# A hybrid decoder layer on one core: spills of a block's split input one transfer at a time, and weight sums paused during three attention projections

## The chip, the cores and the metric

The kernel runs on one core of one Trainium2 chip. Its time is device microseconds (us) of that core; a comparison goes by the median of several runs. PE is TensorE (matmuls), DVE is VectorE, ACT is ScalarE, POOL is GpSimd, SP is SyncE, which here does nothing but issue DMA transfers. POOL issues transfers as well: those that add to what lies at the destination.

## The reference, cut to what matters

One layer of a decoder on 2048 prompt rows and 64 sample rows of width 1024, in float32:

```
h    = rms_norm(x)
proj = h @ w_in                      # q, k, v | z, x/B/C, dt | b, c, u
o_a  = rms_norm(dilated attention(q, k, v))       # three branches, merged
y_b  = rms_norm(ssd_scan(silu(conv(x/B/C)), dt) * silu(z))
y_c  = rms_norm(b * conv(c * u))
x    = x + rms_norm(concat(o_a, y_b, y_c) @ w_out)
f    = relu(rms_norm(x) @ w_mlp_up)**2 @ w_mlp_down
x    = x + rms_norm(f)
# outputs: x of prompt and sample; k and v rows, ssd state, conv states of both
```

## The kernel before, in words

**Products.** Every float32 product of the projections is made of three matmuls on split operands: a value is written as hi + lo (hi rounded to a short format, lo the rest), and hi·lo + hi·hi + lo·hi are added up in one PSUM bank (`mm3`, L282). Weights are split when loaded: ACT writes `whi`, POOL or DVE writes `wlo` (`split_w`). The input rows are split too, once per block: 16 tiles of 128x576 per block (`hi0` to `hi7`, `lo0` to `lo7`), out of a pool of 18 (`hpool`, L356). The tile that comes next in that pool is free once its readers are done.

**Blocks.** The prompt rows are cut into four blocks of 512 (b0 to b3; b0 also carries the sample rows). For a block, `prep` loads its rows (`xt`) and scales them, `build` transposes them on PE, and ACT writes hi and DVE writes lo. Then `in_qkv` makes k, then v, then q, and `in_rest` the remaining columns. The front goes through: b0 qkv, b0 rest, b3 qkv, b2 qkv, b1 qkv, b1 rest, b2 rest, b3 rest. Blocks b3 and b2 are thus needed twice, and the pool holds one block and two tiles: after their split input is built it is written to DRAM (`spill`, L485: 16 transfers of 256 KB into `hT_d`) and read back later (`reload`).

**Inside `in_qkv`** (L548). First k for two column groups (`ks`, reordered copies `kp`, stored to `kL_d`). Then `B.early()` starts `prep` of the next block. Then four tiles of 128 rows: for each, v on PE (`pk`), DVE copies it to `vt` and adds the step sizes into `dtall`; PE turns k (`pkt`), ACT copies it to `kt`; `kt` goes to `out_p_k`, `vt` goes to `v_d` and `out_p_v`, all through SP. I call this the v stage. The tiles `vt` and `kt`, and `yn` of the previous block's end, share one ring of three buffers (tag `s1`): the fourth of them can be written only when the store of the first has landed. Then q for two column groups, ahead of which `B.before_pair()` starts `build` of the next block.

**Weight sums.** The MLP uses sums of quarters of its weights; they are formed in DRAM during the front by transfers alone (`weight_sums`, L1273): of each piece, SP copies a part and POOL adds another to it, six groups a piece, 32 pieces, one group each `SUM_US` (L47).

**Order.** The code runs as Python generators. `PE.us` counts the matmul time issued so far. Other work (`stream`, `advance`) is put in when `PE.us` passes its due time: `poll` (L256) is called at each `yield` of the front. The weight sums have a due time of their own (`behind`). Between what the code issues and what each engine gets stands a scheduler that reorders by its own simulated times; `tc.issue_after(x)` keeps an instruction behind x. Each engine then runs its own list strictly in order, SP's list of transfers too.

Of the kernel before, what the change touches and what calls it, by code (L numbers as in the profile page):

```python
# [10 lines left out]
F32 = mybir.dt.float32  # L11
# [32 lines left out]
HT = 352  # L44
BT = 2 * HT
NSUM = 16
SUM_US = 6.4  # L47
SUM_END = {5: "a13", 7: "a13", 6: "a2", 4: "a4"}
NSP = 14

# [94 lines left out]
def hybrid_layer(ctx: ExitStack, tc: tile.TileContext, I, O, stage=9):  # L145
    nc = tc.nc
    V, A, G, PE, SP = Last(nc.vector), nc.scalar, Last(nc.gpsimd), TimedPE(nc.tensor), Last(nc.sync)
# [8 lines left out]
    hT_d = {b: [dpool.tile([P, 512], F32, name=f"hT_d{b}_{k}") for k in range(2 * KC)] for b in (2, 3)}  # L156
# [33 lines left out]
    def load_gain(psT):  # L190

        rows = cpool.tile([KC, P], F32, name="gprow")
        SP.dma_start(rows, I["norm_mix_pre"][0].rearrange("(k p) -> k p", p=P))
        vp = psT.tile([P, 512], F32, name="vp0", tag="tr")
        PE.transpose(vp[:, :KC], rows, ident[:KC, :KC])
        V.tensor_copy(gpre, vp[:, :KC])

    def load_vectors(psT):
        for r0, n, v in ((V_MLP, 8, I["norm_mlp_pre"][0]),
                         (V_CAT, 2, I["attn_norm"][0]), (V_CAT + 2, 4, I["ssm_norm"][0]),  # L200
                         (V_CAT + 6, 2, I["sconv_norm"][0]), (V_CB, 8, I["ssm_conv_b"][0])):
            SP.dma_start(vrows[r0:r0 + n, :], v.rearrange("(k p) -> k p", p=P))
        SP.dma_start(vrows[V_CW:V_CW + 32, :], I["ssm_conv_w"][0].rearrange("w (k p) -> (w k) p", p=P))
        SP.dma_start(vrows[V_SW:V_SW + 6, :], I["sconv_w"][0].rearrange("w (k p) -> (w k) p", p=P))
        vp = psT.tile([P, 512], F32, name="vp", tag="tr")
        PE.transpose(vp[:, :NV], vrows, ident[:NV, :NV])
        V.tensor_copy(vec, vp[:, :NV])

        V.tensor_scalar(hvec, vec[:, V_CB:V_SW], 0.5, None, op0=ALU.mult)
# [6 lines left out]
    def negate_heads():  # L216
        A.activation(nega, nega, AF.Exp)
        V.tensor_scalar(nega, nega, -1.0, None, op0=ALU.mult)
# [27 lines left out]
    def stream(gen, delay=0.0):  # L246
        streams.append([gen, PE.us + delay])

    def advance(st):
        d = next(st[0], None)  # L250
        if d is None:
            streams.remove(st)
        else:
            st[1] = max(PE.us, st[1]) + d

    def poll():  # L256
        for st in list(streams):
            if PE.us >= st[1]:
                advance(st)
        if behind and PE.us >= behind[1]:  # L260
            sums_on()

    behind = []
    formed = []

    def sums_on():
        d = next(behind[0], None)
        if d is None:
            behind.clear()
        else:  # L270
            behind[1] += d
# [160 lines left out]
    def load_ahead(n):  # L432
        while len(loaded) < min(n, len(plan)):
            while len(raws) < min(len(loaded) + 2, len(plan)):
                load_raw(*plan[len(raws)])
            loaded.append(split_w(raws[len(loaded)]))
# [12 lines left out]
    class Blk:  # L449
# [33 lines left out]
                yield from turn(self.xs[4:], 512, gpre, self.hi, self.lo, pools)  # L483

        def spill(self):  # L485
            for k in range(KC):
                SP.dma_start(hT_d[self.blk][2 * k], self.hi[k][:, :512].bitcast(F32))
                SP.dma_start(hT_d[self.blk][2 * k + 1], self.lo[k][:, :512].bitcast(F32))

        def reload(self):  # L490
            self.hi, self.lo = [], []
# [56 lines left out]
    def in_qkv(B):  # L548
        t0, T = B.t0, B.T

        def rows_out(nm, c, res):

            dst = qL_d if nm == "q" else kL_d
            qs = epool.tile([P, 576], F32, name=f"{nm}s", tag="e0", bufs=3)
            for ps, a, n in res:
                if nm == "q":
                    A.activation(qs[:, a:a + n], ps[:, :n], AF.Copy, scale=E ** -0.5)
                else:
                    A.copy(qs[:, a:a + n], ps[:, :n])
            SP.dma_start(dst[0][:, c, t0:t0 + 512], qs[:, :512])  # L560
            for br, eng in ((1, V), (2, G)):
                dil = BRANCHES[br][1]
                n = 512 // dil
                qp = epool.tile([P, dil, n], F32, name=f"{nm}p{br}", tag="e1" if br == 1 else "xr", bufs=br)
                eng.tensor_copy(qp, qs[:, :512].rearrange("p (i r) -> p r i", r=dil))
                SP.dma_start(dst[br][:, c, :].rearrange("p (r i) -> p r i", r=dil)
                                  [:, :, B.blk * n:B.blk * n + n], qp)
            if B.smp:
                V.tensor_copy((qsm if nm == "q" else ksm)[:, c, :], qs[:, 512:576])
            return qs  # L570

        def use_v(i, t, n, ps):
            vt = epool.tile([P, 256], F32, name="vt", tag="s1", bufs=3)
            V.tensor_copy(vt[:n], ps[:n, :256])
            V.tensor_add(dtall[:n, B.tiles[i][3], :], ps[:n, 256:264], dtb[:n])
            SP.dma_start(v_d[t:t + n, :], vt[:n])
            if t < S:
                SP.dma_start(O["p_v"][0, 0, t:t + n].rearrange("t h e -> t (h e)"), vt[:n])
            else:
                for b in range(NB):  # L580
                    SP.dma_start(O["s_v"][0, b, WB - NS:WB].rearrange("t h e -> t (h e)"),
                                      vt[NS * b:NS * b + NS])

        ksb = []
        yield from B.proj_cols([CK, CK + P], lambda c, res: ksb.append(rows_out("k", (c - CK) // P, res)))
        if B.spilled:
            B.early()
        v_rows = B.proj_tok([(CV, 256), (CDT, HB)], use_v)
        next(v_rows)
        yield  # L590
        for (t, n, a, _) in B.tiles:
            pk = psT.tile([P, 512], F32, name="pkt", tag="tr")
            for c in range(2):
                PE.transpose(pk[:n, c * P:(c + 1) * P], ksb[c][:, a:a + n], ident)
            kt = epool.tile([P, 256], F32, name="kt", tag="s1", bufs=3)
            A.copy(kt[:n], pk[:n, :256])
            if t < S:
                SP.dma_start(O["p_k"][0, 0, t:t + n].rearrange("t h e -> t (h e)"), kt[:n])
            else:
                for b in range(NB):  # L600
                    SP.dma_start(O["s_k"][0, b, WB - NS:WB].rearrange("t h e -> t (h e)"),
                                      kt[NS * b:NS * b + NS])
            next(v_rows)
            yield
        yield from v_rows

        def use_q(c, res):
            rows_out("q", (c - CQ) // P, res)

        if B.spilled:  # L610
            yield from B.proj_cols([CQ, CQ + P], use_q, B.before_pair)
        else:
            for c in range(2):
                yield from B.proj_T(CQ + c * P, use_q)
        B.stage = 1
# [611 lines left out]
    b0, b1, b2, b3 = (Blk(i) for i in range(4))  # L1227
# [45 lines left out]
    def weight_sums():  # L1273
# [22 lines left out]
        for s in range(len(at) + 5):  # L1296
            for k, kind in enumerate(("c13", "a13", "c2", "a2", "c4", "a4")):
                if 0 <= s - k < len(at):
                    group(kind, s - k)
                    formed.append((kind, *at[s - k]))  # L1300
                    yield SUM_US

# [9 lines left out]
    def front():  # L1312
        rows = b0.prep()
        next(rows)
        next(rows)
        SP.dma_start(cst, I["c_main"])
        next(rows)
        load_gain(psT)
        next(rows)
        load_ahead(1)  # L1320
        next(rows)
        load_ahead(3)
        for _ in b0.build():
            pass
        load_vectors(psT)
        load_heads()
        SP.dma_start(abt, I["c_att"])
        load_prev()
        stream(side())
        behind.extend((weight_sums(), PE.us + 30.0))  # L1330
        yield from in_qkv(b0)
        negate_heads()
        stream(ssd_head(b0))
        def then(a, b, build=True):
            a.early = (lambda: stream(b.prep())) if build else (lambda: None)
            a.before_pair = lambda: stream(b.build() if build else b.reload())

        then(b0, b3)
        yield from in_rest(b0)
        b3.spill()  # L1340
        then(b3, b2)
        yield from in_qkv(b3)
        b2.spill()
        then(b2, b1)
        yield from in_qkv(b2)
        yield from in_qkv(b1)
        stream(ssd_head(b1))
        then(b1, b2, False)
        yield from in_rest(b1)
        stream(ssd_head(b2))  # L1350
        then(b2, b3, False)
        yield from in_rest(b2)
        stream(ssd_head(b3))
        b3.early = lambda: stream(transition())
        b3.before_pair = lambda: None
        yield from in_rest(b3)
# [606 lines left out]
```

## Time and profile before

| | |
|---|---|
| median of 3 runs | 2794.55 us (2792.34 to 2804.75) |
| the profiled execution's own time | 2796.83 us |
| its span, first to last instruction | 2794.9 us |
| mean granted TensorE clock | 0.968 |
| PE busy | 2588.7 us (93%) |
| DVE, ACT, POOL busy | 1531.4, 1327.7, 1078.8 us |
| DMA: SP's queue, POOL's queue, share of 16 engines' span | 54.5%, 9.2% |

The front lasts to about 1340 us of the span, the MLP from there to the end. The three `in_qkv` of b3, b2 and b1 lie between about 250 and 430 us. A row of the view by windows gives busy us of each engine (with the count of instructions), the granted clock (PEclk, 1.00 is full), the share of time in which the 16 DMA engines moved data (measured per packet; it can pass 1 a little), and GB/s. In the view of waits a row says which engine, for which output tile, waited for whom: us in total, times, the longest one. In the timeline a bracket holds the idle time just before an instruction and what ended it.

### The profile page before, as it was taken

Reading aid. Unit: us, or ns where it says so; the run is one execution under the profiler, and the core shown is the slowest. Engines: PE = TensorE matmul, PEld = TensorE weight load, DVE = VectorE, ACT = ScalarE, POOL = GpSimd, SP = SyncE. Lnnn points to the kernel's source line nnn. Section 1 sums busy time; section 2 is a strip of 40 time slices with the busy share of each in tenths; the row PEclk is TensorE's granted clock in tenths of the full one; section 3 lists DMA queues with packets and bytes.
Section 4 is the critical chain, followed back from the end, with each engine's and each line's share of the span. In section 5 each row is a group of like instructions: output and inputs, shape, how many; then the busy total and the mean of one; then the engine's idle time right before and its main releaser. Section 6 shows DMA issues by size and latency. Waiting matters only on the chain. (4 is left out here: it accounts for less than half of the span.)

```text
span 2794.9 us, 40722 instructions
## 1 busy us (share of the span) xinstructions
PE 2588.7 (93%) x14329; PEld 2186.8 (78%) x14329; DVE 1531.4 (55%) x2994; ACT 1327.7 (48%) x2776; POOL 1078.8 (39%) x1008
## 2 busy tenths in 40 slices
PE   7998889999899878999899999999999999999996
PEld 6897777877877755567799877689987779998775
DVE  4555436456456465554164466844546684445676
ACT  4534334435436333334446654453764455385434
POOL 4545445444354543334567300166610016661002
PEclk9999989999999989999999999999999999999998
DMA  7777998777677549878777545574434456443443
GB/s 210 218 185 224 276 254 228 199 218 213 173 207 205 152 149 287 266 227 260 233 233 212 140 157 171 145 218 146 166 128 151 149 146 197 162 163 128 128 146 92
DMA packets 426260, 528.26 MB, mean 189 GB/s; under 512 B 65482, under 2 KB 326130, under 8 KB 421448
## 3 DMA queue, kind: packets, MB, share of 16 engines
q1 hardware_dynamic: 411352, 483.45, 54.5%
q0 software_dynamic: 14704, 42.21, 9.2%
q8 instruction: 113, 1.85, 0.3%
q14 instruction: 91, 0.75, 0.1%
HBM read 447.90 MB, written 178.19 MB: 224 GB/s over the span
## 5 line engine op out<-in xcount | busy, mean ns | idle before, releaser
L137 POOL TENSOR_TENSOR wlo<-wraw,whi 128x512 fp32r<-128x512 f32 (+2 forms) x359 | 670.7, 1899 | 555.0 <-ACT whi L417 288.4
L1604 ACT CAST whi<-wraw 128x1024 fp32r<-128x1024 f32 x336 | 351.7, 1049 | 341.4 <-PE pm L118 274.3
L118 PE MATMUL pm<-slo,whi 128*128 128x352 f32 x1344 | 437.9, 327 | 16.1 <-DVE slo L137 10.0
L118 PE MATMUL pm<-shi,wlo 128*128 128x352 f32 x1344 | 433.1, 328 | 7.6 <-POOL wlo L137 7.5
L118 PE MATMUL pm<-shi,whi 128*128 128x352 f32 x1344 | 438.2, 326 | 0.0
L118 PE MATMUL pm<-wlo,shi 128*128 128x512 f32 (+1 forms) x1008 | 400.1, 397 | 1.9 <-ACT shi L1612 1.7
L118 PE MATMUL pm<-whi,shi 128*128 128x512 f32 (+1 forms) x1008 | 398.4, 395 | 0.0
L118 PE MATMUL pm<-whi,slo 128*128 128x512 f32 (+1 forms) x1008 | 338.1, 399 | 17.6 <-DVE slo L137 17.6
L137 DVE TENSOR_TENSOR wlo<-wraw,whi 128x1024 fp32r<-128x1024 f32 (+1 forms) x169 | 206.2, 1220 | 198.1 <-ACT whi L1604 189.1
L118 PE MATMUL pj<-lo,whi 128*128 128x512 f32 (+1 forms) x720 | 273.1, 380 | 17.0 <-ACT xr L631 8.1
L118 PEld LDWEIGHTS pm<-slo,whi 128*128 128x128 f32 x1344 | 256.0, 191 | 19.9 <-DVE slo L137 11.2
L118 PE MATMUL pj<-hi,whi 128*128 128x512 f32 (+1 forms) x720 | 263.1, 365 | 0.0
L118 PEld LDWEIGHTS pm<-shi,wlo 128*128 128x128 f32 x1344 | 255.1, 191 | 9.2 <-POOL wlo L137 8.9
L118 PE MATMUL pj<-hi,wlo 128*128 128x512 f32 (+1 forms) x720 | 262.1, 365 | 0.0
L137 POOL TENSOR_TENSOR ssf<-ssf 128x1 f32<-128x1 f32 (+1 forms) x18 | 6.6, 369 | 647.1 <-ACT jkf L1805 647.0
L118 PEld LDWEIGHTS pm<-shi,whi 128*128 128x128 f32 x1344 | 256.0, 191 | 0.2
L137 DVE TENSOR_TENSOR x<-pm,x 128x352 f32<-128x352 f32 x240 | 123.4, 521 | 222.5 <-PE pm L118 222.4
L118 PEld LDWEIGHTS pm<-whi,slo 128*128 128x128 f32 (+1 forms) x1008 | 179.7, 181 | 76.0 <-DVE slo L137 26.3
L118 PEld LDWEIGHTS pm<-wlo,shi 128*128 128x128 f32 (+1 forms) x1008 | 182.4, 181 | 60.4 <-ACT shi L1612 8.7
L118 PEld LDWEIGHTS pm<-whi,shi 128*128 128x128 f32 (+1 forms) x1008 | 182.0, 181 | 51.2
L1612 ACT CAST shi<-x 128x352 fp32r<-128x352 f32 x288 | 136.9, 484 | 155.0 <-DVE x L137 102.8
L137 DVE TENSOR_TENSOR slo<-x,shi 128x352 fp32r<-128x352 f32 x288 | 157.1, 554 | 35.6 <-ACT shi L1612 30.5
(324 smaller groups left out, 4887.3 us busy)
## 6 DMA issues: line engine op xcount, KB each, us to landing
wraw<-in_w_in SPq DMA_DIRECT2D x192, 256.0 KB
wraw<-u_d SPq DMA_DIRECT2D x96, 512.0 KB
wraw<-d_d SPq DMA_DIRECT2D x96, 512.0 KB
wraw<-in_w_mlp_up SPq DMA_DIRECT2D x72, 512.0 KB
wraw<-in_w_mlp_down SPq DMA_DIRECT2D x72, 512.0 KB
u_d<-in_w_mlp_up POOLq DMA_DIRECT2D x64, 256.0 KB, 5.6
d_d<-in_w_mlp_down POOLq DMA_DIRECT2D x64, 256.0 KB, 7.3
out_s_k<-in_cache_attn_k SPq DMA_DIRECT2D x8, 2040.0 KB
```

Source lines behind the costliest of these rows:

```text
L118: return self.eng.matmul(out, lhsT, rhs, **kw)
L137: out = f(*args, **kw)
L1604: A.copy(hi, raw)
L1612: A.copy(hi, src)
```

## The change

`spill` becomes a generator: each of its 16 transfers is issued behind the last one that SP has been given, then 1.8 us (of `PE.us`) pass to the next. It is a stream that starts 2.0 us after `in_qkv` of its block begins. What is left of it when the q stage begins is issued at once, ahead of the next block's `build`. The weight sums are held (`hold`) from the end of b0's rest to the end of b1's qkv, and `SUM_US` goes from 6.4 to 5.4.

```diff
-SUM_US = 6.4
+SUM_US = 5.4
...
-        if behind and PE.us >= behind[1]:
+        if behind and not hold[0] and PE.us >= behind[1]:
             sums_on()
 
     behind = []
+    hold = [False]
...
         def spill(self):
+
             for k in range(KC):
-                SP.dma_start(hT_d[self.blk][2 * k], self.hi[k][:, :512].bitcast(F32))
-                SP.dma_start(hT_d[self.blk][2 * k + 1], self.lo[k][:, :512].bitcast(F32))
+                for i, x in enumerate((self.hi[k], self.lo[k])):
+                    with tc.issue_after(SP.last):
+                        SP.dma_start(hT_d[self.blk][2 * k + i], x[:, :512].bitcast(F32))
+                    yield 1.8
...
+        def spill_then(a, b):
+
+            out = a.spill()
+            stream(out, 2.0)
+            then(a, b)
+
+            def before_pair():
+                for _ in out:
+                    pass
+                stream(b.build())
+            a.before_pair = before_pair
+
         then(b0, b3)
         yield from in_rest(b0)
-        b3.spill()
-        then(b3, b2)
+        hold[0] = True
+        spill_then(b3, b2)
         yield from in_qkv(b3)
-        b2.spill()
-        then(b2, b1)
+        spill_then(b2, b1)
         yield from in_qkv(b2)
         yield from in_qkv(b1)
+        hold[0] = False
+        behind[1] = PE.us
         stream(ssd_head(b1))
```

What the scheduler makes of it on SP, at the place where b3's k stage ends and its v stage begins. In the names, `xt` are the rows of the next block, `hT_d3_0` to `hT_d3_15` the 16 spills of b3, `yn`, `kt` and `vt` the tiles of the ring of three. Before:

```order
L137 DMA o_d1_104<-ou_2885 128x264
L137 DMA hT_d3_13_96<-lo6_3106 128x512
L137 DMA hT_d3_14_97<-hi7_3128 128x512
L137 DMA hT_d3_15_98<-lo7_3129 128x512
L137 DMA xt1024_3326<-in_x_prompt 128x1024
L137 DMA xt1152_3372<-in_x_prompt 128x1024
L137 DMA xt1280_3401<-in_x_prompt 128x1024
L137 DMA cat_d_101<-yn_3191 128x256
L137 DMA xt1408_3434<-in_x_prompt 128x1024
L137 DMA h0_3866<-in_state_ssm 128x4x128
L137 DMA kL_d0_63<-ks_3271 128x512
L137 DMA cat_d_101<-yn_3217 128x256
```

The same place now:

```order
L137 DMA xt1024_3317<-in_x_prompt 128x1024
L137 DMA xt1152_3364<-in_x_prompt 128x1024
L137 DMA xt1280_3393<-in_x_prompt 128x1024
L137 DMA xt1408_3427<-in_x_prompt 128x1024
L137 DMA cat_d_101<-yn_3180 128x256
L137 DMA hT_d3_0_83<-hi0_3011 128x512
L137 DMA kL_d0_63<-ks_3262 128x512
L137 DMA cat_d_101<-yn_3206 128x256
L137 DMA hT_d3_1_84<-lo0_3012 128x512
L137 DMA kL_d1_64<-kp1_3265 128x4x128
L137 DMA kL_d0_63<-ks_3271 128x512
L137 DMA wraw_3294<-in_w_in 128x4x128
```

All 16 spills stood ahead of the first `xt`; now all four `xt` stand ahead of the first spill, and the spills go between the stores of the k and v stages.

On SP at the end of b3's v stage, now:

```order
L137 DMA hT_d3_6_89<-hi3_3057 128x512
L137 DMA v_d_100<-vt_3499 128x256
L137 DMA out_p_v<-vt_3499 128x256
L137 DMA hT_d3_7_90<-lo3_3058 128x512
L137 DMA hT_d3_8_91<-hi4_3072 128x512
L137 DMA hT_d3_9_92<-lo4_3073 128x512
L137 DMA hT_d3_10_93<-hi5_3094 128x512
L137 DMA hT_d3_11_94<-lo5_3095 128x512
L137 DMA hT_d3_12_95<-hi6_3111 128x512
L137 DMA hT_d3_13_96<-lo6_3112 128x512
L137 DMA hT_d3_14_97<-hi7_3133 128x512
L137 DMA hT_d3_15_98<-lo7_3134 128x512
```

Seven spills go between other transfers, nine in one run behind the last store of `vt`. For b2 three go ahead of the next block's `xt`, five between the stores of the k and v stages, and eight around the last store of `vt` (two just ahead of it, six behind).

On POOL, at b3's v and q stages (`wlo` are the low parts of split weights, `u1_d` to `u4_d` the sums). Before:

```order
L137 DMA u4_d_111<-in_w_mlp_up 32x2048
L137 TENSOR_TENSOR wlo_3310<-wraw_3291,whi_3309 128x512
L137 TENSOR_TENSOR wlo_3516<-wraw_3301,whi_3515 128x512
L137 TENSOR_TENSOR wlo_3520<-wraw_3303,whi_3519 128x512
L137 TENSOR_TENSOR wlo_3530<-wraw_3511,whi_3529 128x512
L137 TENSOR_TENSOR wlo_3534<-wraw_3513,whi_3533 128x512
L137 DMA u1_d_108<-in_w_mlp_up 32x2048
L137 DMA u3_d_110<-in_w_mlp_up 32x2048
L137 TENSOR_TENSOR wlo_3770<-wraw_3523,whi_3769 128x528
```

And now:

```order
L137 TENSOR_TENSOR wlo_3301<-wraw_3282,whi_3300 128x512
L137 TENSOR_TENSOR wlo_3518<-wraw_3292,whi_3517 128x512
L137 TENSOR_TENSOR wlo_3522<-wraw_3294,whi_3521 128x512
L137 TENSOR_TENSOR wlo_3532<-wraw_3513,whi_3531 128x512
L137 TENSOR_TENSOR wlo_3536<-wraw_3515,whi_3535 128x512
L137 TENSOR_TENSOR wlo_3751<-wraw_3525,whi_3750 128x528
```

The transfers of the sums are gone from this stretch; on POOL and on SP the next of them comes in b1's rest.

## The prediction

> **What bounds the kernel now.** I read first the view by windows, to see where PE is not full.
>
> ```profile
> 250.00:300.00 50.00, 36.68 (x220) 31.55 (x219) 16.00 (x36) 19.40 (x42) 24.38 (x33) 0.86 0.94 282
> 300.00:350.00 50.00, 43.41 (x269) 34.83 (x267) 24.03 (x42) 17.51 (x33) 21.82 (x24) 0.95 1.03 298
> 350.00:400.00 50.00, 48.72 (x262) 38.58 (x263) 21.65 (x45) 18.55 (x34) 23.37 (x20) 0.94 0.94 259
> 400.00:450.00 50.00, 42.84 (x207) 35.30 (x206) 27.08 (x64) 17.75 (x37) 27.21 (x29) 0.90 0.92 239
> ...
> 500.00:550.00 50.00, 48.86 (x372) 44.22 (x370) 22.84 (x69) 21.07 (x60) 20.39 (x21) 1.00 0.73 200
> ```
>
> PE is the bound nearly everywhere, but in the 200 us of the three qkv stages that the change touches it idles 28.4 us (200 less the sum of the first numbers), and there alone the transfers are at 0.92 to 1.03 of the DMA engines' time; at 500 us they are at 0.73 and PE is full to 1.1 us. Next, who is waited for, PE's row first, then those behind it (window 200 to 450 us for PE, 236 to 440 us for DVE and ACT):
>
> ```profile
> PE pk L118 <- DVE dtall L137: 14.0, 3, 7.8
> PE pj L118 <- DVE dtall L137: 6.3, 1, 6.3
> PE pkt L122 <- DVE yn L137: 3.9, 1, 3.9
> PE pkt L122 <- ACT kt L596: 3.3, 1, 3.3
> ...
> DVE vt L137 <- DMA out_p_v<-vt: 11.7, 3, 6.7
> DVE yn L137 <- POOL rstd L137: 10.9, 3, 8.1
> DVE vt L137 <- DMA out_p_k<-kt: 10.3, 2, 9.0
> DVE vt L137 <- DMA cat_d<-yn: 6.5, 2, 4.3
> ...
> ACT kt L596 <- DMA out_p_k<-kt: 25.2, 5, 10.0
> ACT jk L324 <- DMA xt<-in_x_prompt: 8.9, 4, 4.0
> ```
>
> PE waits for a PSUM bank that DVE has not emptied (`dtall` is the last read of `pk`); DVE waits for a buffer of the ring of three, whose store has not landed. So the chain ends at the transfers. The stalls in time, on PE's timeline:
>
> ```profile
> 273.29 0.44 PE L122 MATMUL pkt<-cst,ks 128*128 128x128 f32 x2 [3.95 <-DVE yn L137]
> 278.06 0.69 PE L122 MATMUL pkt<-cst,ks 128*128 128x128 f32 x2 [3.26 <-ACT kt L596]
> 284.19 0.59 PE L118 MATMUL pk<-wlo,hi 128*128 128x264 f32 x1 [5.44 <-DVE dtall L137]
> 284.57 0.42 PE L118 MATMUL pk<-whi,hi 128*128 128x264 f32 x1
> ...
> 287.41 0.28 PE L118 MATMUL pk<-whi,lo 128*128 128x264 f32 x1
> 287.54 0.29 PE L118 MATMUL pk<-wlo,hi 128*128 128x264 f32 x1
> ...
> 351.17 0.59 PE L118 MATMUL pk<-wlo,hi 128*128 128x264 f32 x1 [7.75 <-DVE dtall L137]
> 414.59 0.76 PE L118 MATMUL pj<-lo,whi 128*128 128x512 f32 x1 [6.31 <-DVE dtall L137]
> ```
>
> Three stalls, one in each block's v stage: 12.7 us (b3: 3.95 + 3.26 + 5.44), 7.8 us (b2), 6.3 us (b1), 26.8 us together. Each also costs clock: between 284.57 and 287.41 us 13 matmuls (the timeline's rows, of which the first and the last stand above) start 0.22 us apart instead of 0.12 or 0.13, so (2.84 less 13 x 0.125) about 1.2 us a stall are lost behind it.
>
> What fills the transfers, by queue and by issue, in 250 to 430 us:
>
> ```profile
> q1 hardware_dynamic: 71771, 45.95, 85.1%
> q0 software_dynamic: 679, 3.73, 12.3%
> ...
> u_d<-in_w_mlp_up POOLq DMA_DIRECT2D x13, 256.0 KB, 6.7
> ...
> u_d<-in_w_mlp_up SPq DMA_DIRECT2D x8, 256.0 KB
> ...
> u_d<-u_d SPq DMA_DIRECT2D x6, 256.0 KB
> ```
>
> SP's queue moves 45.95 MB in 85.1% of 180 us: 300 GB/s, or 0.87 us for 256 KB. POOL's queue needs 12.3% of 180 us, 22.1 us, for 13 sums: 1.7 us each, twice as much per byte.
>
> **The pause.** It takes 13 POOL sums (22.1 us) and 14 SP sums (14 x 0.87 = 12.2 us) out of this stretch, 34 of the 175 us that its transfers take; no work of PE leaves it. By throughput alone all three stalls could go: 142 us of transfers against 153 us (180 less 27) of PE's work. But stores wait in the crowd of their own v stage, so I count there. The v stages of b3 (262 to 293 us), b2 (325 to 360 us) and b1 (393 to 419 us) have, of POOL's queue:
>
> ```profile
> q0 software_dynamic: 96, 0.52, 11.6%
> ...
> q0 software_dynamic: 144, 0.79, 11.0%
> ...
> q0 software_dynamic: 96, 0.52, 10.7%
> ```
>
> That is 3.6, 3.9 and 2.8 us, and SP issues 1, 3 and 4 sums in them (0.9, 2.6, 3.5 us): 4.5, 6.5 and 6.3 us of transfers ahead of the stores go.
>
> **The spills.** They move 32 x 256 KB before and after; only their place changes. In b3's stage before, all 16 were issued ahead of the rows of the next block:
>
> ```profile
> L137 SPq DMA_DIRECT2D hT_d<-hi x16: 320/460/1161, 240.3 to 326.4; - x16
> ...
> 263.23 1.73 SPq L137 DMA_DIRECT2D xt<-in_x_prompt  x3
> ...
> 270.66 1.06 ACT L324 ACTIVATE jk<-xt 128x1024 bf16<-128x1024 f32 x1 [4.03 <-DMA xt<-in_x_prompt]
> ...
> 342.74 1.04 SPq L137 DMA_DIRECT2D out_p_k<-kt  x1
> ```
>
> The first row was there 7.4 us after its issue; ACT stood for it, POOL computes each `rstd` from ACT's sums in its own order, and DVE's `yn` waited for POOL (up to 8.1 us above), which gives the 3.95 us wait. With `xt` first it comes sooner by up to 4 us, and that wait should go. Against this, seven spills (7 x 0.87 = 6.1 us) now lie between the stores of this very stage, where before only two were issued; before, the others went out from 240 us on, where the queues still had room. So b3's stall changes by 4.5 us of sums and a backlog at 262 us that I bound by 0 and 4 us, against 6.1 us of spills. Bounds of the gain: 0 (spills cancel all else) and 12.7 us. I take 4, the part with `xt`, as the rest nearly balances.
>
> In b2's stage 6.5 us of sums and the tail of the spills (three issued in it, 2.6 us) go, and five spills (4.3 us) come: 4.8 us less ahead of the stores, against a stall of 7.8. Also SP reached the first `out_p_k` of this stage only at 342.74 us; with fewer transfers ahead on SP it gets there earlier. I take 5, bounds 0 and 7.8. In b1's stage no spill lies before or after: 6.3 us of sums against a stall of 6.3 us, less what landed in time anyway; I take 5, bounds 2 and 6.3. Two stalls that nearly vanish bring the clock back twice, 2.4 us, bounds 0 and 3.6.
>
> A rule of the Trainium skill speaks against the spills' new place: "DMA: Bandwidth & Descriptors", Queues, rings and completion order, says that each DMA engine takes the descriptors of one queue's ring in ring order. By it a spill ahead of a store delays that store by the spill's full time, however little SP waits. The time from issue to landing of SP's transfers is not in this trace, so it is not shown here; by the rule alone b3's gain would be 0 and the total below 4 us smaller.
>
> **New runs of spills.** What is left at the q stage goes out at once: nine (7.8 us) for b3, eight (7.0 us) for b2. `build` of the next block writes hi into tiles whose spill must have landed, on ACT, with the weight splits `whi` and the copies of q queued behind. I cost this at nothing, because the two q groups are 48 matmuls of 512 columns, and the k stage that needs the last hi follows them; the timeline has 0.23 us from one such matmul to the next:
>
> ```profile
> 249.30 0.39 PE L118 MATMUL pj<-hi,whi 128*128 128x512 f32 x1
> 249.53 0.39 PE L118 MATMUL pj<-hi,wlo 128*128 128x512 f32 x1
> ```
>
> 48 x 0.23 = 11 us cover 7 to 8 us. If a backlog of more than 3 us stands at that point, the cover is gone (rival two).
>
> **The denser sums.** The 34 us of transfers come back between 430 and 1350 us, at one group per 5.4 instead of 6.4 us.
>
> ```profile
> 430.00:1350.00 920.00, 832.26 (x4700) 648.04 (x4699) 494.36 (x1235) 388.02 (x1074) 401.92 (x507) 0.95 0.74 212
> ...
> PE pt L122 <- DVE ct L137: 6.1, 1, 6.1
> ...
> PE pos L118 <- DMA vn<-in_cache_attn_v: 4.6, 6, 1.3
> ```
>
> 34 of 920 us lift the share from 0.74 to 0.78. The two PE waits there that have a transfer behind them (`ct` is made of the attention rows just loaded) make 10.7 us; if they grow as busy over free does, 0.74/0.26 to 0.78/0.22, that is by a quarter, it costs 2.7 us. I take 3, bounds 0 and 10.7 (doubled).
>
> **Sum.** 4 + 5 + 5 + 2.4 - 3 = 13.4 us off the profiled execution's 2796.83 us; the median of the runs lies 2.3 us below that, at 2794.55, so the forecast is 2781 us. By the stages' bounds alone the gain lies between 2 - 10.7 = -9 us and 12.7 + 7.8 + 6.3 + 3.6 = 30 us.
>
> **Rivals.** One: *all three stalls vanish*, since 34 us of transfers go and only 27 us of stall stand there. For it: 142 us of transfers in 153 us. Against it: the v stages hold nearly only their own stores and loads (q1 alone is at 85.1%). 30 us gain less 3: 2768 us.
>
> Two, the slower one: *the runs of spills hold up `build`*. Place: ACT's write of hi at the start of the q stages of b3 and b2. If 8 us of the v stage's own transfers still stand in the queue there, the last spill lands 16 us after the q stage began, five us after the q matmuls end, and the k stage of the next block, whose transposes, ACT and DVE steps run behind in order, starves for perhaps 8 us, plus 1.2 us of clock, twice: 18 us. With b3's stall unchanged, 5 us gained at b1, none at b2, and 3 us for denser sums it is 18 - 5 + 3 = 16 us slower: 2811 us. It decides from a queue of 3 us on; DMA at 0.92 to 1.03 speaks for it, the missing sums against it.
>
> Three: *it does less than it says*. Over half of the spills (17 of 32) still go out in runs, the others add to the stores' queue, and only the pause in b1 and half of b2's works: 5 + 2.5 + 1.2 - 3 = 6 us, 2789 us.
>
> **Chances.** About 14 us either way, 0.5%, is what a measurement of this kernel can tell from no change. The forecast has 0.46; its spread (5 us up or down) lies across that bound, so 0.27 of it counts as faster and 0.19 as within 0.5%. Rival one has 0.20, faster. Rival three 0.17, within. Rival two 0.17, slower. Faster 0.47, same 0.36, slower 0.17. The range goes from 2764 (rival one with room of 4 us) to 2803, which leaves out most of rival two; the forecast's own range is 2774 to 2789.
>
> **What would show it.** In the changed profile: DMA share in the three qkv stages below 0.9; no `u_d` issue there; PE's `pk` and `pj` waits for `dtall` down from 20.3 us to some 8, with b3's the largest left; the 3.95 us wait for `yn` gone; ACT `jk` less than 5 us behind `xt`. A row "ACT hi <- DMA hT_d" with more than 5 us at PE's cost would show rival two. The forecast is wrong if DMA stays above 0.95 there with the stalls in place, or if waits for `ct`, `vn` or `sz` between 430 and 1350 us grow by more than 10 us.

## The result: 0.7% slower, and where the time went

The changed kernel takes 2816.89 us (median of 7 runs, 2808.89 to 2823.33) against 2794.55 us, a ratio of 1.007 with the interval 1.0047 to 1.0093: slower, 36 us above the forecast and 14 us above its range. The profiled execution of the change took 2810.80 us with a span of 2809.0 us, 14.1 us more than the span before, so the profile shows about two thirds of what the medians differ by.

What the prediction looked at came about. PE's share in the windows of the change (the columns are those of the prediction's first fence):

```profile
250.00:300.00 50.00, 41.07 (x250) 36.13 (x249) 16.45 (x32) 20.15 (x43) 23.44 (x31) 0.90 0.83 254
300.00:350.00 50.00, 46.36 (x279) 36.60 (x277) 28.01 (x55) 19.21 (x37) 20.74 (x20) 0.97 0.89 248
350.00:400.00 50.00, 50.00 (x280) 40.30 (x280) 20.46 (x43) 17.91 (x32) 22.01 (x18) 0.97 0.94 271
400.00:450.00 50.00, 45.60 (x208) 37.55 (x206) 28.34 (x62) 17.54 (x37) 26.75 (x28) 0.93 0.83 213
450.00:500.00 50.00, 40.79 (x224) 32.31 (x223) 32.31 (x78) 27.90 (x66) 18.82 (x25) 0.90 0.73 210
500.00:550.00 50.00, 46.83 (x345) 42.79 (x345) 15.67 (x55) 19.33 (x58) 18.50 (x16) 0.93 0.69 187
```

Up to 450 us PE idles 17.0 us instead of 28.4, the clock is higher in each window, and transfers are at 0.83 to 0.94. But from 500 to 550 us, where PE had been full to 1.1 us at full clock, it now idles 3.2 us at 0.93, and 9.2 us from 450 to 500. The stalls of 2 us or more left in the three v stages, on PE's timeline of the change:

```profile
278.16 0.54 PE L122 MATMUL py<-cst,yt 128*64 128x128 f32 x2 [3.42 <-DVE yn L137]
284.09 0.59 PE L118 MATMUL pk<-wlo,hi 128*128 128x264 f32 x1 [4.96 <-DVE dtall L137]
...
346.66 1.11 PE L122 MATMUL ph<-cst,h 128*128 128x128 f32 x4 [2.01 <-ACT kt L600]
...
405.71 0.56 PE L118 MATMUL pk<-wlo,hi 128*128 128x264 f32 x1 [4.40 <-DVE dtall L137]
```

b3 has 8.4 us (12.7 before), b2 2.0 (7.8) and b1 4.4 (6.3): 12.0 us less. To divide the whole span I use two copies of ACT as marks, the fifth `ks` (b3's k stage begins) and the ninth `qs` (b1's q stage ends). Of the kernel before, and then of the change:

```profile
262.33 0.58 ACT L559 COPY ks<-pj 128x512 f32<-128x512 f32 x1
...
423.12 0.60 ACT L557 ACTIVATE qs<-pj 128x512 f32<-128x512 f32 x1 [0.72 <-PE pj L118]
```

```profile
266.86 0.58 ACT L563 COPY ks<-pj 128x512 f32<-128x512 f32 x1
...
417.83 0.59 ACT L561 ACTIVATE qs<-pj 128x512 f32<-128x512 f32 x1
```

With DVE's fifth and ninth `cu` (one block's rest ends with the fifth, the attention part with the ninth) this gives five stretches, in us:

| stretch | before | change | difference |
|---|---|---|---|
| up to b3's k stage | 262.3 | 266.9 | +4.6 |
| three qkv stages (pause, spills) | 160.8 | 151.0 | -9.8 |
| b1's rest | 153.4 | 172.4 | +19.0 |
| the other blocks' rests | 385.4 | 388.5 | +3.1 |
| out-projection and MLP | 1833.0 | 1830.3 | -2.7 |

The gain is there, and twice as much is lost right behind it. That stretch by windows, before and in the change:

```profile
423.10:576.50 153.40, 145.94 (x878) 121.53 (x878) 88.40 (x229) 73.14 (x184) 73.53 (x80) 0.98 0.77 208
```

```profile
417.80:590.20 172.40, 153.56 (x888) 127.58 (x886) 94.62 (x237) 72.67 (x185) 76.02 (x83) 0.93 0.73 197
```

PE idles 18.8 us instead of 7.5 (+11.4), and by my estimate a clock of 0.93 over 172.4 us loses 12.1 us where 0.98 over 153.4 lost 3.1 (+9.0). Transfers are *less* dense there than before, 0.73 against 0.77. PE's waits of 1.0 us or more in that stretch, on its timeline before:

```profile
457.09 1.13 PE L118 MATMUL ps<-kt,qt 64*128 64x256 f32 x8 [1.18 <-DVE ou L137]
...
480.65 1.14 PE L118 MATMUL ps<-kt,qt 64*128 64x256 f32 x8 [2.00 <-DVE ou L137]
...
548.47 0.43 PE L118 MATMUL po<-vt,ptsb 128*128 128x64 f32 x2 [1.03 <-DVE hn L137]
...
568.78 0.71 PE L118 MATMUL pcb<-xc 128*128 128x128 f32 x4 [1.23 <-DVE hn L137]
```

and in the change:

```profile
455.60 2.08 PE L118 MATMUL ps<-kt,qt 64*128 64x256 f32 x8 [5.24 <-DVE ou L137]
...
472.87 0.44 PE L118 MATMUL po<-vt,ptsb 128*128 128x64 f32 x2 [1.08 <-ACT ptsb L1090]
...
481.61 1.13 PE L118 MATMUL ps<-kt,qt 64*128 64x256 f32 x8 [2.11 <-DVE ou L137]
...
514.02 3.25 PE L118 MATMUL po<-vt,ptsb 128*128 128x64 f32 x14 [3.17 <-DVE ptsb L137]
...
568.97 0.44 PE L122 MATMUL pb<-cst,xc 128*128 128x128 f32 x2 [2.34 <-DVE ptsb L137]
...
577.10 0.71 PE L118 MATMUL pcb<-xc 128*128 128x128 f32 x4 [1.30 <-DVE hn L137]
...
584.61 0.66 PE L122 MATMUL pt<-cst,sc 128*128 128x128 f32 x4 [1.99 <-DVE y L137]
```

Two things are new. First, PE ended b1's q stage 5.3 us sooner (417.83 against 423.12), but its attention unit at 455 us starts only 1.5 us sooner, since it now waits 5.24 us instead of 1.18 for DVE: the gain ran into the next limit, the chain through DVE. DVE itself had just stood 3.75 us for POOL (`xr`) and 3.83 us for a transfer (`bc`, rows of DRAM copied to all 128 partitions); before, it stood there 2.41 us for ACT and 3.68 us for `bc`. Second, there are waits of 2 to 3 us for DVE at 514 and 569 us. A longer wait can cost clock as well, as behind the first one:

```profile
455.60:459.00 3.40, 3.40 (x11) 2.34 (x12) 3.40 (x11) 2.22 (x5) 2.56 (x4) 0.50 0.03 8
459.00:462.50 3.50, 3.50 (x20) 2.92 (x19) 3.43 (x9) 3.50 (x11) 0.20 (x2) 0.97 0.97 226
```

PE is busy from 455.60 us on, yet has half the clock for 3.4 us, 1.7 us of work lost. The Trainium skill, "TensorE: Matmul & The Clock Gate", Part 1: The HAM clock gate, gives this as the rule (half clock after an idle window of about 3.4 us, full clock after a busy one); this row agrees. The length of a wait alone does not give its price here: in the 3.4 us behind the waits of 2.11, 3.17 and 2.34 us at 481, 514 and 569 us the clock was 0.72, 0.50 and 1.00.

What DVE waited for at 480 us (6.42 us) and at 512 us (5.72 us) is the store of an attention unit's result. SP, POOL and DVE on the timeline of the change, in the order of time:

```profile
471.07 1.55 POOL L137 DMA_DIRECT2D u_d<-in_w_mlp_up  x2
...
474.01 0.51 SPq L137 DMA_DIRECT2D o_d<-ou  x1
474.57 1.22 SPq L137 DMA_DIRECT2D u_d<-in_w_mlp_up  x2
476.13 0.72 SPq L137 DMA_DIRECT2D u_d<-u_d  x1
...
480.09 0.42 DVE L137 CUSTOM_DVE_ANT_0 sc<-ps,abt 128x256 f32<-128x256 f32 x1 [6.42 <-DMA o_d<-ou]
```

`scores` of a unit writes its maxima into a tile `ou` of a ring of two, so it must wait until the store of the unit before the last has landed. Here it landed 6.1 us after its issue (474.01 to 480.09), with two sums issued on POOL's queue 3 us ahead of it and three more transfers of sums right behind it on SP's. DVE works in order, so all that was queued behind that `sc` stood as well.

### The profile page after: what moved, and what is told of

Read it like the earlier page. It is cut to its first block, busy times and chain, and to the rows that moved or that the text cites. A ratio compares the mean times of both kernels' runs of the same rounds, so it can differ in the third digit from the quotient of the medians.

```text
span 2809.0 us, 40731 instructions
## 1 busy us (share of the span) xinstructions
PE 2601.3 (93%) x14329; PEld 2192.2 (78%) x14329; DVE 1531.9 (55%) x2994; ACT 1327.0 (47%) x2776; POOL 1080.7 (38%) x1008
## 5 line engine op out<-in xcount | busy, mean ns | idle before, releaser
L118 PE MATMUL pm<-slo,whi 128*128 128x352 f32 x1344 | 437.7, 327 | 19.2 <-DVE slo L137 10.7
L1629 ACT CAST shi<-x 128x352 fp32r<-128x352 f32 x288 | 137.1, 484 | 152.7 <-DVE x L137 100.6
```

What stands on the lines that cost most here:

```text
L118: return self.eng.matmul(out, lhsT, rhs, **kw)
L1629: A.copy(hi, src)
```

## Experiments

Two theories were tried first. *Density*: the sums at 5.4 crowd the transfers, and the loss grows with their bytes per time. *Layout*: the order is written from a model of PE's time, so an edit of the rate or of the start of the sums in the kernel before puts a quarter to nearly a half of SP's 1448 rows elsewhere, and the order before happens to be a good one. A third came out of the traces: the *stores of `ou`*, a ring that is too small.

**The change taken apart.** `s_only` has the spills one at a time, without pause and at the old rate; `h_only` the pause alone; `r_only` the rate alone; `sh` spills and pause at the old rate.

```
r_only:  -SUM_US = 6.4               +SUM_US = 5.4
h_only:  -if behind and PE.us >= behind[1]:
         +if behind and not hold[0] and PE.us >= behind[1]:
         +hold[0] = True   (ahead of b3.spill())
         +hold[0] = False; behind[1] = PE.us   (behind b1's stages)
s_only:  the change without hold[0] = True / False and with SUM_US = 6.4
sh:      the change with SUM_US = 6.4
```

> The spills sent one at a time, the sums as before (6.4, no pause). Theory A (the denser sums at 5.4 crowd the attention stores after the pause, which costs some 20 us; the rest of the change gains 10 us): 2785 to 2795 us, since without the pause the spills alone gain 0 to 6 us. Theory B (any change of the code's order makes the scheduler lay out the b1 rest anew, and that new order costs the 20 us, whatever the transfers do): 2800 to 2815 us, with the loss again between b1's q stage and b2's x stage.

> The pause alone: spills at once as before, sums at 6.4. Theory A: 2780 to 2790 us, the three attention projections gain 5 to 10 us and nothing is denser after. Theory B: 2800 to 2815 us, the gain of the projections is lost again in b1's rest.

> The denser sums alone: SUM_US 5.4, no pause, spills at once. Theory A: slower by 10 to 25 us, 2805 to 2820 us, with longer waits of DVE for o_d stores in b1's rest. Theory B: no fixed sign, anywhere within 15 us of before.

> Spills one at a time and the pause, but the sums at 6.4 after it. Theory A: 2780 to 2790 us, faster than before, since the density is gone. Theory B: like the whole change, 2805 to 2820 us.

Each ratio is to runs of the kernel before on the same chip; the stretches are in us, from the profiles.

| | time, us | ratio to before | interval | qkv stages | b1's rest | end of the attention part |
|---|---|---|---|---|---|---|
| before | 2794.55 | 1 | | 160.8 | 153.4 | 961.9 |
| s_only | 2793.65 | 0.9997 | 0.9985 to 1.0009 | 163.8 | 153.2 | 961.0 |
| h_only | 2788.98 | 0.998 | 0.9965 to 0.9995 | 150.7 | 159.9 | 956.4 |
| sh | 2798.4 | 1.0008 | 0.9993 to 1.0024 | 150.5 | 159.5 | 956.1 |
| r_only | 2822.95 | 1.0099 | 1.0077 to 1.012 | 165.5 | 159.6 | 979.0 |
| change | 2816.89 | 1.007 | 1.0047 to 1.0093 | 151.0 | 172.4 | 978.7 |

The spills do nothing. The pause alone takes 10 us off the qkv stages in each of its kernels, and gives 6 of them back in b1's rest. The step to 5.4 is what costs: alone it is as slow as the whole change. In b1's rest it adds to what the pause costs there: DVE's waits for `o_d` in that stretch are 15.5 us before, 18.0 in h_only, 14.2 in sh, and 29.8 in the change. (The expectation of a_ou3 below measures b1's rest between other marks: 137.1 us before, 155.8 in the change.)

**The rate by itself.** Only `SUM_US` differs from the kernel before: 6.3, 5.9, 6.5 and 7.4.

> The kernel before with SUM_US 6.3 instead of 6.4: the sums are denser by 1.6% only, but the scheduler lays out the front anew (645 of SP's 1448 rows differ, more than with 5.4). Theory A (how densely the sums move data sets the loss): within 4 us of before, since 28 us came with 18.5%. Theory B (the new order sets it): anywhere within 20 us, and away from 0 by more than 5 us.

> The kernel before with SUM_US 5.9, half the way to 5.4. Theory A: slower by 8 to 18 us, half of the 28 us or a little less. Theory B: no order in the three values 6.3, 5.9 and 5.4; as likely faster than before as slower.

> The kernel before with SUM_US 6.5: the sums are thinner by 1.5%. Theory A (density) is bent already by 6.3, which cost 23 us, and 5.9, which cost 7; it says at most 0, so 2790 to 2798 us. Theory B (6.4 is a chosen value at which the scheduler's order happens to be good; any other order with the full sums is worse): 2800 to 2825 us.

> The kernel before with SUM_US 7.4, thinner by 14%. Theory A: faster by up to 10 us in the front, and what of the sums is left over runs into the MLP, so 2785 to 2800 us. Theory B: 2800 to 2825 us.

| us per group | time, us | ratio | interval |
|---|---|---|---|
| 5.4 | 2822.95 | 1.0099 | 1.0077 to 1.012 |
| 5.9 | 2805.5 | 1.0028 | 1.0014 to 1.0043 |
| 6.3 | 2821.59 | 1.0082 | 1.0057 to 1.0108 |
| 6.4 (before) | 2794.55 | 1 | |
| 6.5 | 2808.08 | 1.007 | 1.0045 to 1.0095 |
| 7.4 | 2786.46 | 0.9976 | 0.9964 to 0.9989 |

The loss doesn't follow the dose: 0.1 us to either side of 6.4 costs 0.7 to 0.8%, more than 5.9 does. Density alone can't be the cause.

**The phase alone.** The rate stays and only the first group starts later, by half a period: in the kernel before 33.2 instead of 30.0, in the change 32.7.

```
b_ph33:  -behind.extend((weight_sums(), PE.us + 30.0))
         +behind.extend((weight_sums(), PE.us + 33.2))
a_ph33:  +behind.extend((weight_sums(), PE.us + 32.7))
```

> The kernel before, rate 6.4, but the first group of the sums starts 3.2 us of matmul time (half a period) later: the same transfers at the same rate, only the scheduler's order is another (394 of SP's rows differ). Theory A: within 3 us of before. Theory B: slower by 5 to 25 us.

> The whole change with the first group 2.7 us later (half a period of 5.4); 103 of SP's rows differ from the change's. Theory A: within 3 us of the change, 2812 to 2820 us. Theory B: anywhere from 2795 to 2830 us.

The kernel before so shifted takes 2809.55 us, ratio 1.0071 (1.0056 to 1.0086): a shift that changes no amount of anything costs as much as the change. The change so shifted takes 2820.79 us, 1.0109 (1.009 to 1.0128), with b1's rest at 176.1 us; by the intervals it can't be told from the change. The losses do not sit in one place: in the profiles r63 has 13 of its 17 us in the out-projection and MLP, b_ph33 has 8.4 of its 12 us in the three qkv stages. This speaks for layout, and says that a single number for any of these kernels has some 15 us of luck in it.

**The sums' bytes taken out.** Each transfer of a sum is cut to an eighth of its columns, at 6.4 and at 5.4; the MLP then reads plain quarters of the weights, so the sums are left out of the result.

```
+cut = wsum[m][0].shape[1] // 8
-transfer(SP, o[r], x[r])
+transfer(SP, o[r, :cut], x[r, :cut])
-transfer(G, o[r], x[r], accum_op=ALU.add)
+transfer(G, o[r, :cut], x[r, :cut], accum_op=ALU.add)
```

> The kernel before with each transfer of the weight sums cut to an eighth of its columns (as many transfers, an eighth of the bytes); the MLP reads plain weight quarters in place of the sums, so the sums are left out of what is computed. Theory A: the front runs with 0.05 to 0.1 less DMA share; faster than before by 10 to 40 us. Theory B: within 15 us of before, either side.

> The same cut at SUM_US 5.4. Theory A: as fast as the cut kernel at 6.4 to within 6 us, since the denser transfers now carry an eighth of the bytes; the 28 us of 5.4 are gone. Theory B or a cost that goes by the number of transfers (POOL's and SP's issue time): slower than the cut kernel at 6.4 by 10 to 28 us.

2749.02 us (0.9823, 0.9804 to 0.9842) and 2742.99 us (0.9797, 0.9779 to 0.9815). So the bytes cost 45 to 50 us at 6.4, and 5.4 costs nothing once they are gone: the number of transfers and this new order alone don't hurt. Where they land hurts only while there are bytes in them. In b1's rest the bytes cost nothing at 6.4 (153.9 us without them, 153.4 with them); the profile has 17 us of the gain in the other blocks' rests and 25 us behind them. Of DVE's waits for `o_d` 46.1 of 68.7 us are left at 6.4, so most of them don't hang on these bytes.

**A ring of three.** The largest wait of DVE for a transfer, in the view of waits over the whole kernel, before and in the change (us in total, times, longest):

```profile
DVE sc L137 <- DMA o_d<-ou: 68.7, 23, 12.8
```

```profile
DVE sc L137 <- DMA o_d<-ou: 87.0, 24, 10.5
```

PE hardly shows it: its waits "ps <- DVE ou" are 10.8 and 15.3 us. The direct test is one more buffer, in the kernel before (`b_ou3`) and in the change (`a_ou3`):

```
-self.ou = ou = apool.tile([P, 264], F32, name="ou")
+self.ou = ou = apool.tile([P, 264], F32, name="ou", bufs=3)
```

> The kernel before with a ring of three `ou` tiles. Theory 'stores of ou': its waits for o_d (33.4 us on DVE between 430 and 665 us) go too, of which PE sees little before the change, so the time falls by 0 to 8 us: 2786 to 2795 us. Theory 'crowding' or 'any new order costs': other waits take their place, 2795 to 2815 us.

> The change with a ring of three `ou` tiles in the attention units instead of two; nothing else is edited, though the written order moves in some places with it (141 of SP's 1448 rows). Theory 'stores of ou' (the loss in b1's rest is attention units that stand behind the store of the tile before the last): DVE's waits 'sc <- DMA o_d<-ou' between 425 and 685 us, 47.0 us in the change, fall below 10 us, b1's rest (155.8 us in the change, 137.1 before) comes to 145 us or less, and the time to 2800 to 2807 us. Theory 'crowding' (the transfers are late as a whole, and the ou store is only the first buffer to show it): the o_d waits go, but other waits for transfers (qt, kt2, vt2, bc, raw weights) take their place, b1's rest stays at 150 us or more, and the time at 2812 to 2825 us.

b_ou3 takes 2753.39 us, ratio 0.9848 (0.9827 to 0.9868); a_ou3 2766.54 us, 0.9901 (0.987 to 0.9932). The waits are gone (b_ou3, then a_ou3):

```profile
DVE sc L137 <- DMA o_d<-ou: 2.4, 2, 1.8
```

```profile
DVE sc L137 <- DMA o_d<-ou: 1.8, 2, 1.5
```

This is 42 us (2795.72 for the kernel before on the same chip) and 50 us, far more than I had expected of either (0 to 8, and 10 to 17). Most of the 42 us lie in the other blocks' rests (346.6 us instead of 385.4), 7 in b1's rest. A luckier order is a rival, since the edit moves some rows too; but no complete kernel with a ring of two is below 0.9916, and all four with a ring of three (h74_ou3 and a74_ou3 follow) are at 0.9843 to 0.9901. From the end of b1's q stage to the end of the attention part, the windows of before and of b_ou3:

```profile
423.10:961.90 538.80, 498.20 (x3004) 419.47 (x3004) 287.99 (x745) 248.06 (x680) 246.84 (x280) 0.96 0.72 200
```

```profile
423.30:916.40 493.10, 480.56 (x3002) 407.52 (x3001) 289.14 (x744) 247.87 (x679) 247.43 (x280) 0.99 0.79 218
```

The same work (3004 and 3002 matmuls) with transfers packed to 0.79 instead of 0.72, and PE idles 12.5 us instead of 40.6; the clock, 0.99 over 493.1 us against 0.96 over 538.8, gives another 17 us by the same estimate. So a share of 0.79 hurts no one by itself, and density as a cause falls a second time. In the change, PE's waits of 0.6 us or more in b1's rest are, with the ring of three:

```profile
437.44 0.50 PE L118 MATMUL pj<-lo,whi 128*128 128x512 f32 x1 [1.07 <-ACT xr L635]
...
454.62 2.08 PE L118 MATMUL ps<-kt,qt 64*128 64x256 f32 x8 [5.54 <-DVE ou L137]
...
564.52 1.23 PE L118 MATMUL pcb<-xc 128*128 128x128 f32 x4 [5.16 <-DVE hn L137]
```

(and 0.62 us at 546 us). Those at 482, 514 and 569 us are gone, and b1's rest falls from 172.4 to 159.9 us. b_ou3 has 146.6 us there, so 13 of the 19 us that b1's rest lost stay: the wait at 455 us is still there (b_ou3 has no "ps <- DVE ou" above 0.6 us), and one for `hn` has grown to 5.16 us (1.83 in b_ou3). Behind both stands DVE, in a_ou3, waiting for the transfer of `bc`:

```profile
450.87 0.87 DVE L137 TENSOR_SCALAR bc<-bc,acs 128x128 f32<-128x128 f32 x4 [4.14 <-DMA bc<-acsT_d]
...
561.01 1.07 DVE L137 TENSOR_SCALAR bc<-bc,acs 128x128 f32<-128x128 f32 x5 [10.40 <-DMA bc<-acsT_d]
```

Over b1's rest DVE's waits for `bc` are 11.5 us in the change, 18.6 in a_ou3 and 13.4 in b_ou3: with the ring of `ou` longer, the next transfer on DVE's way holds it. No run tests a remedy for that one. With the ring the change's own loss is 13 us by the medians, instead of 22.

**Pause and rate with and without the ring.** At 7.4, thinner than before: the pause alone (`h74`, and with the ring `h74_ou3`), the whole change (`a74`, `a74_ou3`).

> The pause alone, with spills as before and one group per 7.4 instead of 6.4. If the effects add (density sets the loss): the pause alone was 5.6 us faster and 7.4 alone 6.7 us faster, so 2782 us, ratio 0.996. If the place of each transfer sets it (any new order draws its own stalls, 0 to 28 us): anywhere from 2782 to 2815 us, with the qkv stages again near 150 us and the difference behind them, in b1's rest and in the out-projection.

> The whole change with one group per 7.4 instead of 5.4, thinner than before. If density sets the loss: spills and pause at 6.4 were 2 us slower than before, 7.4 alone 6.7 us faster, so about 2790 us, ratio 0.998, and b1's rest below 140 us. If the place of each transfer sets it: 2790 to 2822 us, with waits for o_d in b1's rest wherever sums lie beside such a store.

> The pause alone, one group per 7.4, a ring of three `ou` tiles. If the pause's 10 us in the qkv stages and the ring's 42 us add, with the thin sums leaving b1's rest at 130 us as in the kernel before with the ring: 2753 less 10 is 2743 us, ratio 0.981. If the ring takes away what the thin sums had gained (both act on the waits for o_d, of which h74 has 56 us against 69): about 2750 us, and if the pause costs what it gains, 2753 to 2762 us.

> The whole change with a ring of three `ou` tiles and one group per 7.4 instead of 5.4. Theory 'the rate is what is left': the 13 us by which the change with the ring is behind go, 2745 to 2753 us, within 5 us of the pause alone with ring and 7.4. Theory 'pause and spills cost it': it stays at 2760 to 2770 us, 8 us or more above the pause alone with ring and 7.4, with b1's rest near 142 us as in the change with the ring.

| | ring of two | interval | ring of three | interval |
|---|---|---|---|---|
| before (6.4) | 2794.55 | | 2753.39, 0.9848 | 0.9827 to 0.9868 |
| change (5.4) | 2816.89, 1.007 | 1.0047 to 1.0093 | 2766.54, 0.9901 | 0.987 to 0.9932 |
| pause alone, 7.4 | 2770.82, 0.9916 | 0.99 to 0.9932 | 2751.06, 0.9843 | 0.982 to 0.9867 |
| change, 7.4 | 2784.96, 0.9956 | 0.994 to 0.9972 | 2758.61, 0.986 | 0.9822 to 0.9898 |

With a ring of two these kernels lie 46 us apart, with three 15 us. h74 is 11 us below the least that I had expected of it (2782 us); no run explains that. With the ring, pause and thin sums together win nothing that can be told (0.9843 against 0.9848): the qkv stages are 14 us shorter in h74_ou3 (147.6 against 161.8), and the stretches behind take it back (b1's rest +3, the other blocks +6, the last stretch +4). Whether the 13 us that the change with ring is behind belong to 5.4 or to pause and spills isn't settled: a74_ou3 lies between, and its interval takes in all of b_ou3's and overlaps a_ou3's.

The fastest kernels here that keep the whole sums are b_ou3, which is the kernel before with one buffer more, and h74_ou3.

## Why the prediction was wrong

- **What bounds the kernel now** was right for the stretch it looked at and stopped there. The windows from 450 us on, and the row of 68.7 us above, were in the trace of before; I read only the waits of the changed stretch and PE's own waits for the rest. A wait of an engine that works in order reaches PE under other names: of the 28 us of PE's idle time that the ring took away, "ps <- DVE ou" named 10.8 at most.
- **The three stalls** came out near the terms: b3 4.3 us (4 forecast), b2 5.8 (5), b1 1.9 (5, below its bound of 2). The stretch won 9.8 us of the 16.4 forecast: the clock's 2.4 us are not seen in it, PE is busy 134.0 us there instead of 132.4. `u_d` has one issue left from 267 to 418 us:

```profile
u_d<-u_d SPq DMA_DIRECT2D x1, 256.0 KB
```

- **The spills**: in the whole time their place is worth nothing (s_only, 0.9997). That b3's term came out near 4 was luck. ACT no longer stood for the rows of x, yet a wait for `yn` stayed (3.42 us at 278 us, against 3.95), where I had said that it would go; what went was the wait for `kt` (3.26 us). Nor does it come from the pause alone: PE's stalls in b3's v stage are 11.4 us in h_only and 11.0 in s_only against 12.7 before, and 8.7 in sh. b2's term is the pause's (no stall of 0.6 us is left there in h_only); b1's stalls do not go with the pause (7.5 us in h_only, 7.6 in sh).
- **The denser sums is the step that failed.** I priced it at 3 us, at most 10.7, by letting the two waits grow that have a transfer right behind them. Measured, the step to 5.4 costs 18 us on top of pause and spills (sh to the change) and 28 us alone (r_only). The two waits did not grow:

```profile
430.00:1350.00 920.00, 824.32 (x4615) 637.80 (x4614) 480.15 (x1221) 379.48 (x1054) 399.29 (x506) 0.94 0.75 216
...
PE pt L122 <- DVE ct L137: 6.0, 1, 6.0
PE pos L118 <- DMA vn<-in_cache_attn_v: 4.0, 3, 1.8
```

  The share is 0.75, not 0.78, and `ct` and `vn` make 10.0 us against 10.7; still PE is busy 8 us less and the clock lower by 0.01, 9 us. In part the loss came through a row that I had not put on the list, DVE's wait for `o_d`: in b1's rest it nearly doubled (15.5 to 29.8 us), and the longer ring takes away 9 of the 22 us. Its price is no function of the share: at 0.1 us more or less per group it is 20 to 23 us (0.7 and 0.82% of 2795). The bound of 10.7 had no ground for the same reason. I also let the new rate act only from 430 us on, though the sums run from 30 us: the stretch up to b3's k stage is 4.6 us longer (266.9, and 267.6 in r_only; 259 to 261 at 7.4). A phase shift alone makes it 267.3 too, and at 6.4 h_only and sh have 264.2 and 265.1, so this part is seen but not explained.
- **The gains were summed as if they reached the end.** The 5.3 us that PE had in hand at 418 us were 1.5 us at 455 us, since the chain through DVE, which feeds PE there and waits for `bc`, had become only that much faster. All kernels with the pause at 5.4 or 6.4 show this wait, and h_only's b1's rest is 6.5 us longer than before.
- **The rivals.** Two, the slower one, put the loss on ACT's `hi` behind the spills; no wait "ACT hi <- DMA hT_d" is in the trace of the change. It had the right sign and the wrong place. In s_only PE does wait 4.11 us for `lo` at that place, but there ACT stood for a transfer of weights (`wraw`, 5.88 us), not for a spill. One and three fell with the sign. My list of what would show the forecast wrong, waits for `ct`, `vn` or `sz`, would have missed what happened.

What stays open: 13 us of the change's loss that the ring doesn't take away, for which the waits for `bc` are a candidate that no run tests; why the last stretch (out-projection and MLP) lies anywhere from 1823 to 1846 us in the kernels with the whole sums, with no order that I can see; and what makes one store land late. Two sums on POOL's queue went out just ahead of the slow one above. In sh the last ones on POOL's queue ahead of the store at that place had ended their issue almost 10 us before it, and it lands 2.9 us after its own issue:

```profile
473.02 0.46 SPq L137 DMA_DIRECT2D o_d<-ou  x1
474.03 3.36 SPq L137 DMA_DIRECT2D wraw<-in_w_in  x2
...
475.96 0.42 DVE L137 CUSTOM_DVE_ANT_0 sc<-ps,abt 128x256 f32<-128x256 f32 x1 [3.28 <-DMA o_d<-ou]
```

The Trainium skill, "DMA: Bandwidth & Descriptors", Queues, rings and completion order, says that one DMA engine takes turns between the queues that have work for it, and takes one queue's transfers in order; by it POOL's two sums would share the engines with the store, and the three that SP issued behind it would not hold it up. The two places agree with that, but two places don't show it, and the wait totals don't rank the kernels: r_only is the slowest and has less of this wait than the kernel before.

```profile
DVE sc L137 <- DMA o_d<-ou: 56.6, 20, 7.3
```

## What to carry to other kernels

Before a small wait is removed, look at the longest waits of every engine that works in order, not only at those that PE shows: one more buffer in a ring whose store lands late was worth 42 us here, where PE's own row for it came to 10.8 us. An edit that moves many transfers at once draws a new layout, so measure a neutral shift beside it (here 0.7%) before its own effect of that size is believed. A gain in one stage is worth what is left of it at the next point where another engine, or a transfer that it waits for, is already the limit.

## What was not expected of the hardware

- The time of one order of transfers against another: the same transfers at the same rate, begun 3.2 us later and so issued in another order, cost 0.7% (1.0071), and 0.1 us per group 0.7 to 0.8%.
- The transfers of a stretch can run at 0.79 of the DMA engines' time with PE idle 2.5% (12.5 of 493.1 us), while at 0.72 with a shorter ring it idles 7.5% (40.6 of 538.8 us): it was not the transfers' share that held the kernel.
- Taking seven eighths of the sums' bytes out (2749.02 us) and adding one buffer with all bytes in (2753.39 us) are worth nearly the same, but not at the same place: the first gains behind the other blocks' rests (25 us) where the second gains nothing, the second 39 us in those rests where the first gains 17.
